# Taking the modulation products two pieces at a time, their matmuls in a fixed unbroken order

## The chip, the cores and the metric

The kernel runs on one core of one Trainium2 chip. The metric is the device time of one execution in microseconds. A core has engines that run side by side, each through its own queue in order: PE (TensorE, matrix products), PEld (PE's weight loads), DVE (VectorE), ACT (ScalarE), POOL (GpSimd) and SP (SyncE, which here issues nearly all DMA transfers).

## The reference

Two groups of tokens, 128 context tokens and 256 latent tokens, pass through two layers with the same code and weights of their own. Each layer is modulated by six vectors, made from a condition of each group:

```python
mod = (jax.nn.silu(cond) @ lp["w_mod"] + lp["b_mod"])[:, None, :]      # w_mod: (1024, 6 * 1024)
sh1, sc1, g1, sh2, sc2, g2 = jnp.split(mod, 6, axis=-1)
h = rms_norm(x, lp["norm1"]) * (1 + sc1) + sh1
o, new_ctx = token_mixers(h, lp, ctx_cache, rope_a, rope_b)
x = x + g1 * o
h = rms_norm(x, lp["norm2"]) * (1 + sc2) + sh2
x = x + g2 * conv_ffn(h, lp)
```

`token_mixers` projects h to the inputs of three mixers and their gates: A, grouped-query attention; B, multi-head latent attention; C, a Hyena long convolution. Their outputs are projected, gated, added and projected once more. `conv_ffn` is a projection up to 2 x 2816 columns, a convolution of width 3, a SiLU gate and a projection down. The change is in the first line alone, the products of `cond` with `w_mod`.

## The kernel before

All 384 tokens are kept as one batch in SBUF, turned so that channels lie on partitions. Each main product is exact to fp32 through a split: a weight is cut into a high and a low part (`hi_lo`: ACT copies the high part, DVE subtracts it), the tokens too, and `mm3` issues three matmuls (lines 269, 270, 271) for one product. An output of 128 columns of a projection from 1024 channels is 8 x 3 = 24 matmuls.

Weights come through two rings. `raw_ring` has 2 buffers of 1 MB, filled by SyncE's DMA (line 249 in `load_w`); from there a weight is split into `hi_ring` and `lo_ring`, which have 4 places each (a 1 MB load fills two). A load waits until the buffer that it takes, two loads back in the ring, has been read: by the split, when a main weight lies in it, and by its matmuls, when a piece of modulation weights lies in it.

The six vectors (v = 0 to 5) of a layer are made by `mod_vec`. A vector's 1024 x 1024 weights come in 4 pieces of 1 MB, of 256 rows (`mod_load`, line 329). For each piece PE runs 4 matmuls (line 338) of 32 columns each, side by side on the four column strips of its array (`tile_position`), in fp32, which the trace shows as two instructions each: x8 is a piece. They add into one PSUM bank; when all pieces are in, ACT copies the bank, PE transposes it (line 302), DVE adds the bias. `mod_vec` is a generator: it yields after each piece, after the copy, and at the end, so a vector is 4 + 2 steps. Some pieces are loaded ahead into other buffers (`ready`); the others go through `raw_ring`: 16 pieces of layer 0 (v = 2 to 5), and in layer 1 two of v = 0 and 1, four of v = 3 and four of v = 4.

`weave(main, (line, rate), ...)` takes a step of the main line and then, for each side line, adds the rate to a counter and takes a step when the counter reaches 1; the counters start at zero in each call. The modulation line `md` has rate R_MD. In each layer the main lines are, in order: the two halves of `hyena_in` (12 and 13 steps; three loads each), `attn_proj` (24 steps, nine matmuls to a step, six loads with the columns in widths of 512, 448 and 480), and then gates (16 steps, four loads) and branch (8 steps, four loads of 512 KB) for mixers 2, 0 and 1. Beside them run the Hyena chain `ch` up to the end of `attn_proj`, and the attention line `att` in gates and branches. `finish(md)` takes what is left before the output projection.

What the generators give is program order. Each engine's own order is fixed when the kernel is built: an instruction that is ready goes by priority, which is program order unless `tc.high_priority(offset=...)` raises it. `tc.issue_after(ins)` lets an instruction go to its engine only behind `ins`. The attention outputs (line 954) use both already:

```python
with ExitStack() as order:
    order.enter_context(tc.high_priority(offset=U_AV))
    if last is not None:
        order.enter_context(tc.issue_after(last))
    last = pe.matmul(p[b:b + 64, u], v, pT, start=start, stop=stop, tile_position=(0, b)).ins
```

Of the kernel before, what the change touches and what calls it, by code (L numbers as in the profile page):

```python
# [15 lines left out]
KD = 8  # L16
# [12 lines left out]
PI_C = TWO_PI - PI_A - PI_B  # L29
MAGIC = 12582912.0  # L30
ATT_LAG = 3
R_MD, R_FL, R_CH = 0.24, 2, 0.8
R_AT = 0.8, 0.9, 0.9, 1, 2
R_FL2, R_AH = 0.45, 0.5
PS_HY0 = {"mm": "123", "tr": "46", "fl": "05"}
# [11 lines left out]
U_AV = 2000  # L47
# [138 lines left out]
def kernel(  # L186
# [8 lines left out]
    act, dve, pool, pe, sp = nc.scalar, nc.vector, nc.gpsimd, nc.tensor, nc.sync  # L195
# [11 lines left out]
    def banks(**lines):  # L207

        for line, own in lines.items():
            turns[line] = [int(b) for b in own]  # L210

    def ps_of(line, *shape):
        own = turns[line]
        own.append(b := own.pop(0))
        n = 1
        for d in shape:
            n *= d
        v = all_banks[:, b, 0:n]
        if len(shape) == 1:
            return v  # L220
        return v.rearrange("p (a b) -> p a b", a=shape[0])
# [8 lines left out]
    def copy_a(out, in_, scale=1.0):  # L230
        act.activation(out=out, in_=in_, func=AF.Copy, scale=scale)  # L231
# [5 lines left out]
    def tt(out, a, b, op):  # L237
        dve.tensor_tensor(out=out, in0=a, in1=b, op=op)  # L238

    def stt(out, a, s, b, op0, op1):  # L240
        dve.scalar_tensor_tensor(out=out, in0=a, scalar=s, in1=b, op0=op0, op1=op1)  # L241

    raw_ring = Ring(base, 2, 2048)
# [41 lines left out]
    cT = base.alloc(KD, 32).ap()  # L285
# [14 lines left out]
    def transpose(out, in_):  # L300
        n = in_.shape[0]
        pe.transpose(out, in_, ident[:n, :n])  # L302
# [23 lines left out]
    def mod_load(l, v, k, buf):  # L326
        raw = buf.ap(2, 1024)
        src = w_mod[l, k * 256:(k + 1) * 256, v * 1024:(v + 1) * 1024]
        sp.dma_start(out=raw, in_=src.rearrange("(k p) n -> p k n", p=128))
        return raw  # L330

    def mod_vec(l, v, ready=(), bufs=()):

        gv = ps_of("md", 512)
        for k in range(KD // 2):
            raw = ready[k] if k < len(ready) else mod_load(l, v, k, raw_ring.get())
            for j in range(4):
                pe.matmul(  # L338
                    gv[32 * j:32 * j + 32], cT[:, 2 * k + j // 2], raw[:, j // 2, (j % 2) * 512:(j % 2) * 512 + 512],
                    start=k == 0, stop=k == KD // 2 - 1, tile_position=(0, 32 * j),  # L340
                )
            if bufs:
                bufs.pop(0).free()
            yield
        ms = mod_s
        copy_a(ms.ap(), gv)
        yield
        pm = ps_of("md", 4, 128)
        for q in range(4):
            transpose(pm[:, q], ms.ap()[:, q * 128:(q + 1) * 128])  # L350
        sums_of = pm.rearrange("p q (h j r) -> p h j q r", h=2, r=32)[:, :, :, :, 0:2]
        out = mods[l][:, v * 8:v * 8 + 8].rearrange("p (j q) s -> p j q s", q=4)
        bias = vecs[l][:, V_B + v * 8:V_B + v * 8 + 8].rearrange("p (j q) -> p j q", q=4)
        tt(out, sums_of[:, 0], bias.unsqueeze(3).to_broadcast([128, 2, 4, 2]), ALU.add)
        tt(out, out, sums_of[:, 1], ALU.add)
        if v in (1, 4):
            o = (V_N1, V_N2)[v // 4]
            g = vecs[l][:, o:o + 8].unsqueeze(2).to_broadcast([128, 8, 2])
            stt(avs[l][:, v // 4], mods[l][:, v * 8:v * 8 + 8], 1.0, g, ALU.add, ALU.mult)
        yield  # L360
# [895 lines left out]
    nxt = []  # L1256
# [36 lines left out]
    class Ahead:  # L1293


        def __init__(self, l, vs, n):
            ready = {v: [] for v in vs}
            bufs = {v: [] for v in vs}

            def loads():  # L1300
                for v, k in [(v, k) for v in vs for k in range(KD // 2)][:n]:
                    bufs[v].append(FA.alloc(2048, top=True))
                    ready[v].append(mod_load(l, v, k, bufs[v][-1]))
                    yield

            self.loads = loads()
            self.steps = chain(*[mod_vec(l, v, ready[v], bufs[v]) for v in vs])
# [36 lines left out]
    def chain(*lines):  # L1344
        for g in lines:
            yield from g
# [27 lines left out]
    ready = [mod_load(0, 0, k, early[k]) for k in range(2)]  # L1374
# [6 lines left out]
    for k in range(4):  # L1381
        ready.append(mod_load(0, 1, k, early[4 + k]))
    act.activation(out=cT[:, :, 0:2], in_=cT[:, :, 0:2], func=AF.Silu)
    weave(chain(mod_vec(0, 0, ready[:4]), mod_vec(0, 1, ready[4:])), (fl, R_F0), (squares(), 1.2))
    for b in early_parts:
        b.free()
    parts = split_slab.whole(F32R).cut(1024)
# [9 lines left out]
        sp.dma_start(out=rope_b[:, i], in_=rt[:, 128:192].rearrange("p (a b) -> p a b", a=2))  # L1397
    sp.dma_start(out=vecs[1], in_=p_vec[1])
    for l in range(NL):
        md = chain(*[mod_vec(l, v) for v in (2, 3, 4, 5)]) if l == 0 else chain(nxt.pop().steps, mod_vec(l, 4))  # L1400
        banks(**PS_HY0)
        weave(main, (md, R_MD), (fl, R_FL))
        finish(fl)
# [199 lines left out]
```

## Time and profile before

| | |
|---|---|
| time, median of 3 runs | 1503.31 us (1502.71 to 1505.6) |
| the profiled execution: time | 1507.35 us |
| its span, first to last instruction | 1505.2 us |
| its mean granted TensorE clock | 0.992 |
| PE busy | 1460.2 us, 97% of the span |
| DVE, ACT busy | 1005.3 us (67%), 750.7 us (50%) |
| HBM traffic over the span | 140 GB/s |

Busy time is time in which an instruction of the engine runs; matmuls overlap in the engine's pipeline, so a matmul's own duration is longer than its distance from the next. The granted clock is a share of TensorE's full speed, 2.4 GHz. In the lists, `banks` is PSUM, `base` the slab with the raw ring, `split` the slab with the split weights, `s` the slabs of temporary tiles; out<-in names what is written and read.

### The profile page before, as it was taken

Reading aid. Unit: us, or ns where it says so; the run is one execution under the profiler, and the core shown is the slowest. Engines: PE = TensorE matmul, PEld = TensorE weight load, DVE = VectorE, ACT = ScalarE, POOL = GpSimd, SP = SyncE. Lnnn points to the kernel's source line nnn. Section 1 sums busy time; section 2 is a strip of 40 time slices with the busy share of each in tenths; the row PEclk is TensorE's granted clock in tenths of the full one; section 3 lists DMA queues with packets and bytes.
Section 4 is the critical chain, followed back from the end, with each engine's and each line's share of the span. In section 5 each row is a group of like instructions: output and inputs, shape, how many; then the busy total and the mean of one; then the engine's idle time right before and its main releaser. Section 6 shows DMA issues by size and latency. Waiting matters only on the chain.

```text
span 1505.2 us, 22120 instructions
## 1 busy us (share of the span) xinstructions
PE 1460.2 (97%) x8574; PEld 1342.2 (89%) x8574; DVE 1005.3 (67%) x1920; ACT 750.7 (50%) x1376; POOL 97.1 (6%) x125
## 2 busy tenths in 40 slices
PE   5799999999999999999999999999999999999997
PEld 3589889989889899999997888999888989999997
DVE  5758569547447886686775766884655777567674
ACT  4644456455444663454545444855555464344343
POOL 0222210000000000000000212100000000000000
PEclk9899999999999999999999999999999999999999
DMA  9444354434466542343266345332333533433431
GB/s 366 146 134 157 135 164 140 114 105 126 140 211 233 191 134 95 125 126 128 85 226 220 124 142 180 103 102 88 90 122 114 184 110 113 139 102 122 156 116 52
DMA packets 177496, 212.84 MB, mean 141 GB/s; under 512 B 24176, under 2 KB 160112, under 8 KB 177392
## 3 DMA queue, kind: packets, MB, share of 16 engines
q1 hardware_dynamic: 176528, 206.99, 42.6%
q0 software_dynamic: 864, 4.46, 0.9%
q8 instruction: 67, 1.10, 0.3%
q14 instruction: 37, 0.30, 0.1%
HBM read 209.29 MB, written 2.13 MB: 140 GB/s over the span
## 4 chain that ended last, share of the span: by engine, by line
PE 92%; DVE 3%; ACT 2%; DMA 1%; issue 1%; SPq 0%; DVEq 0%; ACTq 0%
PE banks L269 27%; PE banks L270 26%; PE banks L271 26%; PE banks L302 3%; PE banks L338 3%; PE banks L922 3%; DVE s L238 2%; PE banks L954 2%; PE banks L558 1%; DMA base<-in_w_in_dram 1%; DVE split L235 1%; PE banks L503 1%; ACT s L231 1%; PE banks L538 0%; DMA s<-in_p_w_dram 0%
## 5 line engine op out<-in xcount | busy, mean ns | idle before, releaser
L231 ACT ACTIVATE split<-base 128x1024 fp32r<-128x1024 f32 (+2 forms) x272 | 280.8, 1040 | 374.1 <-PE banks L270 264.1
L235 DVE TENSOR_TENSOR split<-base,split 128x1024 fp32r<-128x1024 f32 (+2 forms) x272 | 332.0, 1225 | 181.4 <-ACT split L231 180.8
L269 PE MATMUL banks<-h,split 128*128 128x384 f32 x1280 | 432.9, 342 | 5.2 <-DVE h L403 3.6
L270 PE MATMUL banks<-h,split 128*128 128x384 f32 x1280 | 435.9, 341 | 0.3
L271 PE MATMUL banks<-h,split 128*128 128x384 f32 x1280 | 433.2, 339 | 0.0
L269 PEld LDWEIGHTS banks<-h,split 128*128 128x128 f32 x1280 | 241.4, 189 | 19.5 <-issue 8.4
L270 PEld LDWEIGHTS banks<-h,split 128*128 128x128 f32 x1280 | 242.1, 189 | 4.6 <-issue 1.6
L271 PEld LDWEIGHTS banks<-h,split 128*128 128x128 f32 x1280 | 241.6, 189 | 2.4 <-issue 0.7
L270 PE MATMUL banks<-s,split 128*128 128x384 f32 x672 | 225.8, 337 | 0.0
L271 PE MATMUL banks<-s,split 128*128 128x384 f32 x672 | 225.6, 338 | 0.0
L269 PE MATMUL banks<-s,split 128*128 128x384 f32 x672 | 223.2, 339 | 1.0 <-ACT s L231 0.8
L241 DVE SCALAR_TENSOR_TENSOR s<-banks,base,s 128x127 f32<-128x127 f32 (+1 forms) x448 | 172.6, 411 | 8.4 <-ACT s L417 4.3
L231 ACT ACTIVATE s<-banks 128x384 f32<-128x384 f32 (+11 forms) x212 | 94.4, 472 | 101.3 <-PE banks L271 38.7
L231 ACT ACTIVATE s<-s 128x384 fp32r<-128x384 f32 (+3 forms) x142 | 79.0, 562 | 103.9 <-DVE s L238 57.6
L269 PEld LDWEIGHTS banks<-s,split 128*128 128x128 f32 x672 | 125.6, 188 | 4.4 <-ACT s L231 1.4
L271 PEld LDWEIGHTS banks<-s,split 128*128 128x128 f32 x672 | 126.1, 188 | 2.0 <-DVE base L241 0.8
L270 PEld LDWEIGHTS banks<-s,split 128*128 128x128 f32 x672 | 126.2, 188 | 1.4 <-issue 0.2
L238 DVE TENSOR_TENSOR s<-banks,s 128x512 f32<-128x512 f32 (+3 forms) x132 | 81.6, 645 | 43.7 <-PE banks L271 18.8
L241 DVE SCALAR_TENSOR_TENSOR base<-banks,base 128x128 f32<-128x128 f32 (+1 forms) x128 | 46.9, 412 | 74.8 <-PE banks L271 74.8
L238 DVE TENSOR_TENSOR s<-s 128x256 f32<-128x256 f32 (+4 forms) x122 | 68.0, 568 | 23.6 <-ACT s L1225 8.3
L302 PE MATMUL banks<-base,s 128*128 128x128 f32 x442 | 75.3, 274 | 2.3 <-DVE s L241 1.3
L417 ACT ACTIVATE s<-banks,base 128x384 f32<-128x384 f32 x112 | 73.2, 655 | 7.1 <-PE banks L271 7.1
(145 smaller groups left out, 1729.7 us busy)
## 6 DMA issues: line engine op xcount, KB each, us to landing
base<-in_w_in_dram SPq DMA_DIRECT2D x40, 1024.0 KB, 5.4
base<-in_ffn_up_dram SPq DMA_DIRECT2D x40, 1024.0 KB, 5.2
base<-in_w_mod_dram SPq DMA_DIRECT2D x28, 1024.0 KB, 5.2
s<-in_w_mod_dram SPq DMA_DIRECT2D x14, 1024.0 KB, 7.5
base<-in_ffn_down_dram SPq DMA_DIRECT2D x16, 896.0 KB, 5.0
base<-in_w_branch_dram SPq DMA_DIRECT2D x24, 512.0 KB, 3.5
base<-in_w_out_dram SPq DMA_DIRECT2D x8, 1024.0 KB, 5.4
base<-in_ffn_down_dram SPq DMA_DIRECT2D x8, 1024.0 KB, 5.3
```

The costliest lines, as they stand in the source:

```text
L231: act.activation(out=out, in_=in_, func=AF.Copy, scale=scale)
L235: dve.tensor_tensor(out=lo, in0=src, in1=f(hi), op=ALU.subtract)
L238: dve.tensor_tensor(out=out, in0=a, in1=b, op=op)
L241: dve.scalar_tensor_tensor(out=out, in0=a, scalar=s, in1=b, op0=op0, op1=op1)
L269: pe.matmul(out, l[0], r[0], start=start, stop=False)
L270: pe.matmul(out, l[0], r[1], start=False, stop=False)
L271: pe.matmul(out, l[1], r[0], start=False, stop=stop)
L302: pe.transpose(out, in_, ident[:n, :n])
L338: pe.matmul(gv[32 * j:32 * j + 32], cT[:, 2 * k + j // 2], raw[:, j // 2, (j % 2) * 512:(j % 2) * 512 + 512], start=k == 0, stop=k == KD / ...
L417: act.activation(out=dst, in_=src, func=AF.Identity, scale=vec(l, w1), bias=vec(l, bias))
L922: pe.matmul(out, q_of(h)[:, i * 128:(i + 1) * 128], k, start=m == 0, stop=m == len(ks) - 1)
L954: last = pe.matmul(p[b:b + 64, u], v, pT, start=start, stop=stop, tile_position=(0, b)).ins
```

## The change

`mod_vec` gets a parameter `pieces`. With `pieces=2` it loads two pieces in one step and issues their 8 matmuls in one go, the piece that was loaded last first. In every call, also with one piece, the matmuls of a step go through `in_turn`: each but the first has its priority raised by U_AV = 2000 and is put behind the one before it. `pieces=2` is used for v = 2 to 5 of layer 0 and v = 4 of layer 1, where the line runs beside the main lines; R_MD goes from 0.24 to 0.16, as such a vector now takes 2 + 2 steps.

```diff
--- before.py
+++ after.py
@@ -29,7 +29,7 @@
 PI_C = TWO_PI - PI_A - PI_B
 MAGIC = 12582912.0
 ATT_LAG = 3
-R_MD, R_FL, R_CH = 0.24, 2, 0.8
+R_MD, R_FL, R_CH = 0.16, 2, 0.8
 R_AT = 0.8, 0.9, 0.9, 1, 2
 R_FL2, R_AH = 0.45, 0.5
 PS_HY0 = {"mm": "123", "tr": "46", "fl": "05"}
@@ -329,16 +329,34 @@
         sp.dma_start(out=raw, in_=src.rearrange("(k p) n -> p k n", p=128))
         return raw
 
-    def mod_vec(l, v, ready=(), bufs=()):
+    def in_turn(parts):
+
+        last = None
+        for part in parts:
+            with ExitStack() as order:
+                if last is not None:
+                    order.enter_context(tc.high_priority(offset=U_AV))
+                    order.enter_context(tc.issue_after(last))
+                last = part().ins
+
+    def mod_vec(l, v, ready=(), bufs=(), pieces=1):
 
         gv = ps_of("md", 512)
-        for k in range(KD // 2):
-            raw = ready[k] if k < len(ready) else mod_load(l, v, k, raw_ring.get())
-            for j in range(4):
-                pe.matmul(
-                    gv[32 * j:32 * j + 32], cT[:, 2 * k + j // 2], raw[:, j // 2, (j % 2) * 512:(j % 2) * 512 + 512],
-                    start=k == 0, stop=k == KD // 2 - 1, tile_position=(0, 32 * j),
-                )
+
+        def part(k, j, raw, first, last):
+            return pe.matmul(
+                gv[32 * j:32 * j + 32], cT[:, 2 * k + j // 2], raw[:, j // 2, (j % 2) * 512:(j % 2) * 512 + 512],
+                start=first, stop=last, tile_position=(0, 32 * j),
+            )
+
+        for k0 in range(0, KD // 2, pieces):
+            ks = range(k0, k0 + pieces)
+            raws = [ready[k] if k < len(ready) else mod_load(l, v, k, raw_ring.get()) for k in ks]
+            own = list(zip(ks, raws))[::-1]
+            in_turn([
+                lambda i=i, k=k, j=j, raw=raw: part(k, j, raw, k0 + i == 0, k0 + i == KD // 2 - 1)
+                for i, (k, raw) in enumerate(own) for j in range(4)
+            ])
             if bufs:
                 bufs.pop(0).free()
             yield
@@ -1397,7 +1415,10 @@
         sp.dma_start(out=rope_b[:, i], in_=rt[:, 128:192].rearrange("p (a b) -> p a b", a=2))
     sp.dma_start(out=vecs[1], in_=p_vec[1])
     for l in range(NL):
-        md = chain(*[mod_vec(l, v) for v in (2, 3, 4, 5)]) if l == 0 else chain(nxt.pop().steps, mod_vec(l, 4))
+        if l == 0:
+            md = chain(*[mod_vec(l, v, pieces=2) for v in (2, 3, 4, 5)])
+        else:
+            md = chain(nxt.pop().steps, mod_vec(l, 4, pieces=2))
         banks(**PS_HY0)
         weave(main, (md, R_MD), (fl, R_FL))
         finish(fl)
```

## Rows read from the trace of the kernel before

**Rows 1.** Part 1 of the page: busy time, share of the span, instructions of each engine.

```profile
PE 1460.2 (97%) x8574; PEld 1342.2 (89%) x8574; DVE 1005.3 (67%) x1920; ACT 750.7 (50%) x1376; POOL 97.1 (6%) x125
```

**Rows 2.** Part 4 of the page: the chain that ended last, shares by line.

```profile
PE banks L269 27%; PE banks L270 26%; PE banks L271 26%; PE banks L302 3%; PE banks L338 3%; PE banks L922 3%; DVE s L238 2%; PE banks L954 2%; PE banks L558 1%; DMA base<-in_w_in_dram 1%; DVE split L235 1%; PE banks L503 1%; ACT s L231 1%; PE banks L538 0%; DMA s<-in_p_w_dram 0%
```

**Rows 3.** Stages: window and length, busy us by engine (x instructions), granted clock, DMA share, GB/s.

```profile
142.00:207.00 65.00, 65.00 (x342) 51.31 (x341) 41.45 (x65) 24.25 (x45) 20.21 (x20) 1.00 0.48 156
...
367.00:430.00 63.00, 63.00 (x362) 51.33 (x361) 30.76 (x73) 30.98 (x72) 0.00 (x0) 1.00 0.41 125
```

**Rows 4.** The chain that ended last, in order of time: start us, us, what (x instructions).

```profile
95.70 0.98 PE banks L338 x4
...
388.76 3.18 PE banks L954 x32
...
836.82 0.97 PE banks L338 x2
840.25 0.99 PE banks L338 x6
...
1207.05 3.57 PE banks L338 x32
```

**Rows 5.** PE's timeline around a lone modulation piece: start us, us, engine line op.

```profile
117.49 0.33 PE L270 MATMUL banks<-h,split 128*128 128x384 f32 x1
117.67 0.34 PE L271 MATMUL banks<-h,split 128*128 128x384 f32 x1
117.94 1.06 PE L338 MATMUL banks<-base 128*32 128x512 f32 x8
118.93 0.45 PE L269 MATMUL banks<-h,split 128*128 128x384 f32 x1
119.21 0.34 PE L270 MATMUL banks<-h,split 128*128 128x384 f32 x1
```

**Rows 6.** Source line L338: what its engine sat idle for (us, times).

```profile
  DMA base<-in_w_mod_dram: 0.9, 2
```

**Rows 7.** Waits of SyncE's queue: who for whom, us in total, times, longest.

```profile
SPq L249 <- DVE split L235: 460.4, 74, 20.7
...
SPq L249 <- PE banks L338: 68.2, 15, 8.6
```

**Rows 8.** The chain in order of time again, behind the modulation run at 321.44.

```profile
322.49 5.56 DMA base<-in_w_in_dram
...
329.10 1.05 ACT split L231
```

**Rows 9.** DMA issues, 437.2 to 437.8: tile, queue, count, KB each, median us to landing.

```profile
base<-in_w_out_dram SPq DMA_DIRECT2D x2, 1024.0 KB, 6.6
```

**Rows 10.** Stages again: the projection's second width (layer 0), its third (layer 1).

```profile
163.11:182.79 19.68, 19.68 (x112) 16.30 (x111) 10.64 (x16) 7.06 (x15) 6.65 (x6) 1.00 0.55 193
...
923.56:943.72 20.16, 20.16 (x112) 17.95 (x110) 16.11 (x25) 9.60 (x21) 3.63 (x5) 1.00 0.51 147
```

**Rows 11.** Part 5 of the page, the weight split on DVE: busy, mean ns, idle before.

```profile
L235 DVE TENSOR_TENSOR split<-base,split 128x1024 fp32r<-128x1024 f32 (+2 forms) x272 | 332.0, 1225 | 181.4 <-ACT split L231 180.8
```

**Rows 12.** DMA issues of the attention projection, layer 0, 142 to 207.

```profile
base<-in_w_mod_dram SPq DMA_DIRECT2D x4, 1024.0 KB, 5.2
```

**Rows 13.** Groups of instructions in the projection's third width, layer 1: busy, mean ns, idle.

```profile
L269 PE MATMUL banks<-s,s 128*128 128x256 f32 x12 | 3.5, 288 | 0.0
```

**Rows 14.** Stages again: PE's busy time and clock around three waits.

```profile
810.00:814.00 4.00, 2.54 (x16) 1.36 (x9) 4.00 (x10) 3.50 (x8) 0.00 (x0) 1.00 1.03 397
814.00:818.00 4.00, 4.00 (x26) 2.91 (x25) 3.71 (x9) 4.00 (x11) 0.00 (x0) 1.00 0.95 270
826.00:830.00 4.00, 2.15 (x13) 1.67 (x11) 3.98 (x8) 3.64 (x5) 0.00 (x0) 1.00 0.63 204
830.00:834.00 4.00, 4.00 (x15) 3.91 (x15) 3.48 (x8) 0.00 (x0) 1.73 (x3) 0.57 0.70 250
328.00:332.00 4.00, 3.55 (x19) 2.89 (x18) 2.77 (x6) 3.87 (x6) 0.00 (x0) 1.00 0.44 75
```

## The prediction

> **What bounds the kernel now.** Begin with the busy times: TensorE (PE) works in 97% of the span [rows 1], and the chain that ended last lies on PE nearly throughout, 79% of it on the three products of the split matmul and 3% on the modulation matmuls, L338 [rows 2]. The table by stage says how tight that is: in the attention projection of layer 0 PE is busy for 65.00 us of 65.00, in the last gates and branch of that layer for 63.00 of 63.00 [rows 3]. In these stages one microsecond less of PE work is one microsecond less of time, and one microsecond in which PE waits for a weight is lost. Both happen here, so the question is what each weighs.
>
> A modulation piece is 4 matmuls, shown as 8 instructions. The chain in order of time has one row for each unbroken run of them [rows 4]. Look at how little the length depends on the count: a run of 2 takes 0.97 us, one of 4 0.98, one of 6 0.99, and a run of 32, four whole pieces, 3.57. So a piece that other matmuls break in two is paid twice. The row of a first half (x4 at 95.70) is the first of these, the piece at 836.82 and 840.25 the last; counted over the list, 16 rows hold no multiple of 8 (x2 to x6, and one x28), they stand for 7 broken pieces, and there are 9 runs more than there need be.
>
> The PE timeline around a lone piece (x8) gives the whole price of a run [rows 5]: matmuls follow each other every 0.18 us (117.49 to 117.67), the last one before the run is followed after 0.27, the run holds PE for 0.99 (117.94 to 118.93), the first matmul behind it for 0.28 (to 119.21). That is 0.09 + 0.99 + 0.10 = 1.18 us, and 1.17 for half a piece. A further piece inside a run costs (3.57 - 0.99) / 3 = 0.86 us.
>
> **The change part by part.**
>
> Chaining. Each piece's or pair's matmuls follow one another without a break; the same device already holds the 32 instructions of the attention outputs together (L954, one row, 3.18 us [rows 4]), so I take it that it works. 9 runs x 1.17 = 10.5 us less. It cannot gain more; it gains nothing if the breaks remain.
>
> Pairing. 16 pieces of layer 0 and 4 of layer 1 become 10 runs of two. Two lone runs cost 2.36, one run of two 1.18 + 0.86 = 2.04: 0.32 each, 3.2 us in all. With the chaining 13.7 us. That a run's first matmul must now wait for the piece loaded last I price at nothing: over all runs PE's weight loads waited 0.9 us for a modulation load [rows 6], and the weights already split cover the rest.
>
> R_MD. A vector took 4 + 2 steps and takes 2 + 2, and 0.24 x 4/6 = 0.16: 25 main steps for a vector as before. No instruction is added, no load grows; ACT's copy and DVE's adds are the same. I price this at nothing: finish(md) keeps one step instead of two in layer 0.
>
> The weight ring. This is what the change costs. The ring has two 1 MB buffers. SyncE's load of the next weight waits for the vector split of the last one (74 times) or for a modulation run (15 times) [rows 7]. A single piece holds one buffer and leaves the other to the main weights; a pair holds both until its matmuls have run, and no weight behind it can start before. Its matmuls stand where program order puts them, so the weights at hand are then those already split. What a late load costs is seen at 322.49, where w_in waited for L338: 5.56 us for the load, then ACT's split of 1.05 before the first matmul [rows 8]. With 0.1 between them I take 6.7 us from a run's end to the next weight. Two such loads issued together land after 6.6 us in the median of the two [rows 9]; if the first takes the 5.5 of a lone one, the second takes 7.7.
>
> Counting the steps of the weave (the counter starts at zero in each call, a step every 6.25), the pairs fall: v2 at step 7 of either half of hyena_in, v3 (layer 0) and v4 (layer 1) at steps 13 and 19 of the attention projection, v4 in layer 0 at step 7 of branch 2 and of gates 0, v5 at steps 7 and 13 of gates 1.
>
> hyena_in: behind the pair stand at least 2.5 outputs of 24 matmuls, whose weights are already loaded. At 0.18 us a matmul these are 10.8 us, more than 6.7. Nothing is lost.
>
> Attention projection, both layers. It has six loads a0 to a5 of four steps each. A step took (19.68 - 2 x 1.2) / 8 = 2.2 us in the second width and 20.16 / 8 = 2.5 in the third [rows 10]. Call the end of the pair at step 13 X. Three steps of a3 are left (6.5 us); a4 is usable at X + 6.7, or at X + 8.9 if the other freed buffer, the one that the reversed order frees first, is filled ahead of it: PE loses 0.2 to 2.4. The next pair's second piece needs a4's buffer, free after both halves are split (two splits of ACT and the last of DVE at 1.2 [rows 11]: X + 5.6 + 3.3 = 8.9). It lands 5.2 us later [rows 12], at X + 14.1; PE ends step 19 at 6.7 + 3 x 2.5 = X + 14.2. The run of 2.0 ends at X + 16.2, and only then a5 may be loaded: usable at X + 22.9. PE has one step left, to X + 18.7, so it lacks 4.2 us; if the run comes one step later, 6.7. Behind this wait are a5's four steps, the copies of the projection, and all of the attention that reads them. What can fill it is the Hyena chain: 12 groups of three matmuls in the 20 us of this stage, 3.5 us for the first of each three [rows 13], tied to VectorE step by step. I let it fill 0.7 of the lesser wait, and take 3.5 us at a5 and 0.3 at a4 for each layer.
>
> Branch 2, gates 0, gates 1 at step 7. One output, or half of one, is left (2 us and the attention beside it), so 6.7 us leave 2 to 4 open. But at 322.49 the same wait cost PE 0.45 us (3.55 busy in the four from 328 [rows 14]), as the attention line filled the rest. I take 0.3 each, 0.8 together; the far end is 3 x 3 = 9 with no cover. Gates 1 at step 13 has 1.5 outputs left and a load of half the size: nothing.
>
> The clock. A wait has an afterpay. PE was idle for 1.46 us in 810 to 814 and its granted clock stayed at 1.00 (2.4 GHz) in the next 4; it was idle for 1.85 in 826 to 830 and got 0.57 in the next 4 us, most of them at the lower level of 1.2 GHz, which is 1.7 us of work lost [rows 14]. Whether a gap that the Hyena chain breaks up does the same these rows don't tell; between 0 and 1.7 I take half, 0.8 a layer. The Trainium skill (TensorE: Matmul & The Clock Gate, "HAM oscillation — how this bites in real kernels") says that a PE that waits for a DMA between bursts drops to the half clock and begins each burst cold. By that rule both waits would pay in full, and the sum below would be -1.9 us instead of -3.7; the row at 826 agrees with it, the one at 810 doesn't.
>
> Sum: -10.5 - 3.2 + 2 x (3.5 + 0.3 + 0.8) + 0.8 = -3.7 us. The profiled execution took 1507.35 us for a span of 1505.2; it becomes 1503.65. The median of the runs is 1503.31, 4.04 below that execution, and becomes 1499.6.
>
> **The rivals.**
>
> The waits are covered. If the Hyena chain and the next stage's ready work fill the attention projection's gaps too, what is left of the losses is 0 to 7 us and the time 1489.6 to 1496.6. For it: PE found work through nearly all of the wait at 322.49. Against: that was among attention heads; in the projection all later work needs a5.
>
> Gain and loss cancel: losses of 10.7 to 16.7 us, 1500.3 to 1506.3. The clock's full price (+1.8) alone leads here, 1501.4; it is what the Trainium skill's rule above gives. With it 2 us more at a4 in each layer make it no change at all.
>
> Slower: the wait for a5 and its like. With 6.7 unfilled at a5, 2.4 at a4 and 1.7 for the clock a layer pays 10.8, both 21.6, and with the 0.8 the whole is +8.7: 1512. It decides from 8 us a layer on, where the losses pass 16.7. The place is width three of the projection, in both layers.
>
> The change does not do what it says: matmuls of others still break the runs. Then the pairing's 3.2 stand against waits of 10: +6.8, 1510. L954's unbroken runs speak against it.
>
> **How the numbers follow.** About 0.2%, 3 us, is what a measurement of this kernel tells from no change. Forecast (losses of 7 to 10.7, 1496.6 to 1500.3): 0.28. Covered: 0.22. Cancelled: 0.26. Slower by waits: 0.21. Runs still broken: 0.03. So faster 0.50, same 0.26, slower 0.24. Cases of both signs hold much, so the range goes far to either side, 1490 to 1509: it leaves out the upper half of the slower cases, some 0.13, and little of the covered one, some 0.05. The forecast's own is 1496.6 to 1500.3.
>
> **What would show it.** Right: in the chain 10 rows of x16 near 1.9 us and no L338 row under x8 in the weaves; PE idle for 3 to 4 us before L269 late in the projection of each layer, ended by an ACT split behind a w_in load that waited for L338; a granted clock below 1.00 there. Wrong: runs still broken (the 10.5 gone); no idle time in the projection (then nearer 1490); idle time of over 8 us a layer, or new gaps in gates 0 and 1 (then slower); a modulation run that itself waits for its second piece.

## The result and the profile after

The changed kernel takes 1525.19 us (median of 4 runs, 1523.86 to 1529.78); beside it the kernel before took 1504.05 (4 runs, 1502.71 to 1505.6). The ratio is 1.0140 with a 95% interval of 1.0128 to 1.0153, so the change makes the kernel 21 us slower. The forecast was 1499.6 in a range of 1490 to 1509: the direction was wrong, and the time lies 16 us beyond the far end. The profiled execution of the changed kernel has a span of 1523.4 us against 1505.2, 18.2 more. Line numbers move: the modulation matmuls of L338 are now L347, the attention outputs of L954 are L972.

Start where the prediction started, with the busy times and the chain (part 1 of the page, the chain's lines of part 4, and of the groups by line the four of the modulation matmuls: busy us, mean ns, idle before):

```profile
PE 1458.2 (96%) x8574; PEld 1348.4 (89%) x8574; DVE 1000.6 (66%) x1920; ACT 744.2 (49%) x1372; POOL 98.7 (6%) x125
...
PE banks L269 26%; PE banks L270 25%; PE banks L271 25%; PE banks L302 3%; DMA base<-in_w_in_dram 2%; PE banks L940 2%; PE banks L347 2%; DVE s L238 2%; PE banks L972 2%; DVE split L235 1%; ACT split L231 1%; ACT s L231 1%; PE banks L576 1%; PE banks L521 1%; DVE s L241 1%
```

```profile
L347 PE MATMUL banks<-base 128*32 128x512 f32 x224 | 30.1, 632 | 0.0
L347 PE MATMUL banks<-s,base 128*32 128x512 f32 x112 | 13.1, 596 | 0.0
L347 PE MATMUL banks<-split,base 128*32 128x512 f32 x32 | 4.3, 604 | 0.0
L347 PE MATMUL banks<-h,base 128*32 128x512 f32 x16 | 2.1, 605 | 0.0
```

The gain is there. The same four groups of L338 had 39.4, 13.9, 4.3 and 2.1 us before, together 59.7; now they have 49.6. That is 10.1 less, and the 44 runs on PE have become 27: at the 0.19 us around a run that the forecast read from [rows 5], 17 x 0.19 = 3.2 more. So 13.3 us of PE work went, where 13.7 were forecast. But against [rows 1] PE's busy time fell by 2.0 alone, and span less busy time, PE's idle time, rose from 45.0 to 65.2. In the chain against [rows 2], transfers of w_in have gone from 1% to 2% and stand ahead of the attention outputs. Two things ate the gain: waits for weights, and matmuls that run at a lower clock behind them.

The stages say where (columns as in [rows 3]; boundaries are the first projection matmul of each stage). First the kernel before: the projection of layer 0, gates 0 with its branch in layer 0, the projection of layer 1.

```profile
141.84:210.10 68.26, 68.26 (x362) 54.31 (x362) 42.84 (x70) 26.93 (x51) 20.37 (x20) 1.00 0.50 162
...
272.30:343.62 71.32, 69.54 (x450) 62.05 (x450) 33.37 (x69) 37.33 (x76) 0.45 (x3) 1.00 0.41 114
...
882.42:943.72 61.30, 61.30 (x336) 51.46 (x334) 38.35 (x58) 25.08 (x47) 12.35 (x16) 1.00 0.55 178
```

Then the changed kernel: in layer 0 hyena_in, the projection, gates 0 with its branch, and all gates and branches together; in layer 1 hyena_in, the projection, gates and branches.

```profile
65.01:140.41 75.40, 75.34 (x450) 69.06 (x449) 50.64 (x99) 39.47 (x72) 17.62 (x22) 0.98 0.41 133
140.41:214.94 74.53, 68.90 (x371) 57.18 (x369) 43.59 (x73) 26.21 (x50) 14.38 (x19) 0.95 0.50 160
...
277.55:358.67 81.12, 71.69 (x440) 64.20 (x440) 36.12 (x70) 39.26 (x76) 0.45 (x3) 0.94 0.37 103
...
214.94:509.89 294.95, 282.93 (x1730) 253.38 (x1728) 177.35 (x351) 151.17 (x312) 5.06 (x9) 0.98 0.47 148
...
825.64:891.74 66.10, 63.87 (x392) 59.34 (x393) 48.73 (x96) 34.56 (x61) 12.97 (x18) 1.00 0.44 142
891.74:965.75 74.01, 68.32 (x371) 56.27 (x369) 42.00 (x69) 26.10 (x50) 16.18 (x18) 0.95 0.47 149
965.75:1233.13 267.38, 263.01 (x1623) 246.35 (x1623) 172.72 (x341) 148.25 (x306) 3.84 (x7) 1.00 0.39 118
```

| stage (PE idle in brackets), us | before | after |
|---|---|---|
| hyena_in, layer 0 | 75.99 (0) | 75.40 (0.1) |
| attention projection, layer 0 | 68.26 (0) | 74.53 (5.6) |
| gates and branches with the output projection, layer 0 | 285.55 (1.8) | 294.95 (12.0) |
| of these gates 0 and its branch | 71.32 (1.8) | 81.12 (9.4) |
| hyena_in, layer 1 | 70.24 (2.0) | 66.10 (2.2) |
| attention projection, layer 1 | 61.30 (0) | 74.01 (5.7) |
| gates and branches with the output projection, layer 1 | 272.16 (5.4) | 267.38 (4.4) |

PE did not wait at all in either projection before. Now it waits 5.6 us in each, and its granted clock there has fallen from 1.00 to 0.95. In layer 0 the rest of the loss lies in gates 0 and its branch, which take 9.8 us more; the other gates and branches of that layer give 0.4 us back.

**Layer 1's projection, one wait.** The chain in order of time, with three modulation runs ahead of it (start us, us, what; compare [rows 4]):

```profile
126.29 1.85 PE banks L347 x16
...
402.96 0.98 PE banks L347 x2
...
407.12 1.88 PE banks L347 x14
...
944.67 1.04 PE banks L347 x8
945.73 5.49 DMA base<-in_w_in_dram
951.24 1.06 ACT split L231
952.33 1.30 DVE split L235 x2
```

A pair is one run of 16 instructions in 1.85 us. Only one of the ten is broken, at 402.96, where the attention outputs came in behind its first matmul, which is not raised in priority. Now look at the run at 944.67: the transfer at 945.73 is released by its first half, eight instructions. The half that runs first reads the piece loaded last, so the buffer taken last comes free first. The two loads issued behind this run (issues from 945.6 to 946.2 and from 946.4 to 947; KB, us to landing):

```profile
base<-in_w_in_dram SPq DMA_DIRECT2D x1, 1024.0 KB, 5.5
...
base<-in_w_in_dram SPq DMA_DIRECT2D x1, 960.0 KB, 7.0
```

The 960 KB are a5, the last weights of this projection, and needed first. The 1024 KB are the first weights of the gates, needed later. They go first and land in 5.5 us; a5 is issued at 946.59, shares the transfer engines with them, and takes 7.0. PE and ACT show the end of it (start us, us, engine line op, in brackets the idle time before):

```profile
944.60 1.92 PE L347 MATMUL banks<-base 128*32 128x512 f32 x16
...
950.50 0.28 PE L271 MATMUL banks<-s,s 128*128 128x256 f32 x1
954.67 1.57 PE L269 MATMUL banks<-split,h 128*128 128x480 f32 x3 [3.89 <-ACT split L231]
```

```profile
951.24 2.00 ACT L231 ACTIVATE split<-base 128x1024 fp32r<-128x1024 f32 x2 [2.50 <-DMA base<-in_w_in_dram]
...
953.62 1.90 ACT L231 ACTIVATE split<-base 128x960 fp32r<-128x960 f32 x2
```

ACT splits the weights that nobody waits for (128x1024) and then a5's (128x960). The run ends at 944.60 + 1.85 = 946.45; PE's first matmul with a5 is at 954.67, 8.2 us later. In layer 0 the same pair of loads goes out at 193.63 (1024 KB) and 194.49 (960 KB, again 7.0 us), and there ACT's split of the gates' weights ran from 199.11 on, two copies followed, and a5's split came at 202.06.

**Gates 0 of layer 0** show another form of the same hold. SyncE's queue (start us, us, line, x transfers):

```profile
279.92 0.37 SPq L329 DMA_DIRECT2D base<-in_w_mod_dram  x1
282.78 3.03 SPq L1081 DMA_DIRECT2D base<-in_mla_w_uq_dram  x6
...
314.37 0.37 SPq L329 DMA_DIRECT2D base<-in_w_mod_dram  x1
321.28 1.43 SPq L1081 DMA_DIRECT2D base<-in_mla_w_uq_dram  x3
322.76 0.49 SPq L249 DMA_DIRECT2D base<-in_w_in_dram  x1
```

The pair's first piece takes one ring buffer at 279.92 and holds it until the run at 320.19, for 40 us. The other goes to weights of the attention line (line 1081), which are split only just before 314.37; then the second piece is loaded. Behind it in the queue stand the attention line's next weights and w_in, which go out at 321.28 and 322.76. Before, w_in had gone out at 287.42 and the second part of w_uq at 298.07. Over the whole run loads of line 249 wait for a modulation run 19 times, 22.8 us at the longest; in [rows 7] it was 15 times and 8.6 us. The total is 67.6 against 68.2 us, so what tells is where the waits fall. The wait is in PE's timeline (the row at 322.98 is the last work before it):

```profile
322.98 0.60 PE L302 MATMUL banks<-base 128*128 128x128 f32 x4
329.82 0.69 PE L269 MATMUL banks<-h,split 128*128 128x384 f32 x1 [6.24 <-ACT split L231]
```

In the kernel before, PE spent the same wait for w_in (from 322.49 on, [rows 8]) on the matmuls of this second part of w_uq, 27 of the following kind, and its weights had come through the ring at 298.07:

```profile
323.43 0.34 PE L269 MATMUL banks<-s,s 128*128 128x384 f32 x1
```

Here too the clock falls with the wait. Windows of 4 us behind the waits of layer 0's projection, of gates 0 and of layer 1's projection, columns as before; the first number behind the length is PE's busy time, the third from the end its clock (compare [rows 14]):

```profile
200.00:204.00 4.00, 1.82 (x5) 1.30 (x5) 3.80 (x5) 3.94 (x6) 0.65 (x1) 0.60 0.35 106
204.00:208.00 4.00, 4.00 (x17) 3.69 (x16) 3.07 (x5) 0.38 (x1) 0.00 (x0) 0.55 0.98 272
...
324.00:328.00 4.00, 0.00 (x0) 0.00 (x0) 0.24 (x2) 0.00 (x0) 0.00 (x0) 0.88 0.98 286
328.00:332.00 4.00, 2.18 (x6) 1.74 (x7) 2.20 (x2) 3.06 (x3) 0.00 (x0) 0.50 0.21 44
332.00:336.00 4.00, 4.00 (x20) 4.00 (x19) 1.43 (x2) 0.00 (x0) 0.00 (x0) 0.76 0.67 183
...
948.00:952.00 4.00, 2.16 (x13) 1.55 (x12) 1.56 (x5) 1.39 (x2) 0.07 (x1) 0.96 1.06 384
952.00:956.00 4.00, 1.33 (x3) 1.05 (x4) 3.67 (x5) 3.41 (x5) 0.00 (x0) 0.50 0.27 86
956.00:960.00 4.00, 3.98 (x14) 3.03 (x13) 2.09 (x3) 0.00 (x0) 0.00 (x0) 0.68 0.98 277
```

0.50 is the lower level, 1.2 GHz. An estimate of what it costs is the busy time of a window times the missing share of its clock: 0.73 + 1.80 = 2.5 us behind the wait in layer 0's projection, 1.09 + 0.96 = 2.1 in gates 0, and 0.09 + 0.67 + 1.27 = 2.0 in layer 1's projection.

### The profile page after: what moved, and what is told of

Read it like the earlier page. It is cut to its first block, busy times and chain, and to the rows that moved or that the text cites. A ratio compares the mean times of both kernels' runs of the same rounds, so it can differ in the third digit from the quotient of the medians.

```text
span 1523.4 us, 22120 instructions
## 1 busy us (share of the span) xinstructions
PE 1458.2 (96%) x8574; PEld 1348.4 (89%) x8574; DVE 1000.6 (66%) x1920; ACT 744.2 (49%) x1372; POOL 98.7 (6%) x125
## 4 chain that ended last, share of the span: by engine, by line
PE 88%; DVE 4%; DMA 3%; ACT 3%; issue 1%; POOL 0%; SPq 0%; DVEq 0%; ACTq 0%; POOLq 0%
PE banks L269 26%; PE banks L270 25%; PE banks L271 25%; PE banks L302 3%; DMA base<-in_w_in_dram 2%; PE banks L940 2%; PE banks L347 2%; DVE s L238 2%; PE banks L972 2%; DVE split L235 1%; ACT split L231 1%; ACT s L231 1%; PE banks L576 1%; PE banks L521 1%; DVE s L241 1%
## 5 line engine op out<-in xcount | busy, mean ns | idle before, releaser
L235 DVE TENSOR_TENSOR split<-base,split 128x1024 fp32r<-128x1024 f32 (+2 forms) x272 | 328.1, 1211 | 173.0 <-ACT split L231 172.3
L238 DVE TENSOR_TENSOR s<-banks,s 128x512 f32<-128x512 f32 (+3 forms) x132 | 81.5, 646 | 44.7 <-PE banks L271 21.7
L235 DVE TENSOR_TENSOR s<-s,s 128x384 fp32r<-128x384 f32 (+2 forms) x102 | 62.8, 619 | 28.3 <-ACT s L231 20.7
```

What stands on the lines that cost most here:

```text
L235: dve.tensor_tensor(out=lo, in0=src, in1=f(hi), op=ALU.subtract)
```

## The experiments

The main theory: a pair holds both ring buffers until its run, and the reversed order then gives the buffer of the less urgent load back first. Rivals: the chaining itself costs (raised priority, matmuls put behind one another); the slower pace or the two steps in one do; or one stage alone pays. Each ratio is to the kernel before, timed on the same chip, whose median was 1504.87 for the first four runs, 1504.22 for the next four and 1505.74 for the last two.

**Chaining alone.** All pieces single, in their runs unbroken.

```diff
-R_MD, R_FL, R_CH = 0.16, 2, 0.8
+R_MD, R_FL, R_CH = 0.24, 2, 0.8
...
-            md = chain(*[mod_vec(l, v, pieces=2) for v in (2, 3, 4, 5)])
+            md = chain(*[mod_vec(l, v) for v in (2, 3, 4, 5)])
...
-            md = chain(nxt.pop().steps, mod_vec(l, 4, pieces=2))
+            md = chain(nxt.pop().steps, mod_vec(l, 4))
```

> Each piece alone as before (one piece to a step, R_MD 0.24), but its matmuls chained. Theory (the loss is the ring held by pairs): PE's time in modulation runs falls by some 9 of the 69.6 us of the kernel before, PE's idle time stays near 32 us, and the time is 1504 - 10 = 1494 us (1490 to 1497). Rival (the chaining itself does the harm, by pulling modulation matmuls ahead of work that the chain of the end needs): 1510 to 1525. Second rival (the new order of the schedule alone moves the time by up to 1%): anywhere from 1494 to 1515, with idle time in other places than after.

Measured: 0.9979 (0.9969 to 0.9988), 1501.87 us. The modulation matmuls take 50.8 us in 36 runs, 8.9 less, and with 8 x 0.19 around the runs 10.4 less: the forecast's term for the chaining, 10.5, is right as PE work. (The 69.6 and 32 us that the expectation gives for the kernel before are 59.7, or 68.1 with the 0.19 around each run, and 45.0 in its trace.) As time it is not: the expected 1490 to 1497 was missed. PE's idle time rose from 45.0 to 47.6 and the span fell by 6.0 (to 1499.2); the median fell by 3.0 alone (1.8 to 4.7 by the interval), as the traced execution of the kernel before lies 2.5 us above its median (1507.35 against 1504.87). So the chaining by itself doesn't cost, but of 10.4 us of PE work it gives some 3 us of time.

**Pairs in loading order.** The reversal is taken out.

```diff
-            own = list(zip(ks, raws))[::-1]
+            own = list(zip(ks, raws))
```

> The changed kernel, but a pair's matmuls go in the order of loading, so that the buffer of the piece loaded first comes free first, and with it the load that PE needs first. Theory (part of the loss is that the weight needed second is loaded and split ahead of the one needed first): in the projection of each layer a5 is loaded first, PE resumes 1.5 to 3 us earlier, in both layers together with the clock 4 to 8 us less, 1517 to 1521 us. Rival (the order of loading makes no difference, both loads go together): 1524 to 1526. If the run now breaks after the first piece, because the second has not landed, the gain is smaller and single runs show.

Measured: 0.9996 (0.9987 to 1.0006), 1504.07 us. One slice costs 21.7 us (1.0140 against 0.9996). The time is far below the 1517 to 1521 expected. Layer 0's projection takes 64.09 us with no idle time. Layer 1's is still long, with 2.95 us of idle time; there the pair at 923.23 came as one run of 16.

```profile
874.29:942.39 68.10, 65.15 (x366) 54.51 (x364) 40.31 (x66) 26.45 (x50) 17.26 (x19) 1.00 0.50 162
```

Two things change at once, though: in loading order the first piece's matmuls can run as soon as it has landed, so its buffer comes back before the second piece is even in, and the order of the freed buffers is mended. The hold-forward run below parts them.

**Pairs in loading order, not chained.**

```diff
-                if last is not None:
-                    order.enter_context(tc.high_priority(offset=U_AV))
-                    order.enter_context(tc.issue_after(last))
...
-            own = list(zip(ks, raws))[::-1]
+            own = list(zip(ks, raws))
```

> Pairs as in the changed kernel, in the order of loading, without the chain (no raised priority, no issue order). Theory (the ring alone makes the loss): the idle time of the changed kernel in the projections and gates 0 stays (some 15 to 20 us over before), the modulation runs break again and cost 6 to 12 us more than in the changed kernel: 1527 to 1535 us. Rival (the chain makes the loss): 1500 to 1510.

Measured: 1.0048 (1.0031 to 1.0065), 1511.27 us; the modulation matmuls are back at 59.1 us. Against the run before, the chaining is worth 7.8 us among pairs. Pairing without it is a loss, but a smaller one than the expected 1527 to 1535: the expectation had counted on the changed kernel's idle time, most of which is not there in loading order (50.2 us in all, against 65.2).

**Pairs as changed, the second piece in a buffer of its own.** The order within the run and its wait for both pieces stay; in nine of ten pairs the second piece goes into a free place of the activations' memory instead of the ring.

```diff
+OWN_FROM = 1
...
-            raws = [ready[k] if k < len(ready) else mod_load(l, v, k, raw_ring.get()) for k in ks]
...
+                    if pieces == 2 and k > k0 - 1 + OWN_FROM:
+                        try:
+                            b = FA.alloc(2048, top=True)
...
+                    if b is None:
+                        b = raw_ring.get()
+                    else:
+                        held.append(b)
+                    raws.append(mod_load(l, v, k, b))
```

> The changed kernel, but the second piece of each pair lies in a buffer of its own from the arena, wherever there is room for 1 MB (9 of the 10 pairs; not the first of v = 4 in layer 0), so that a pair holds one buffer of the weight ring, as a single piece does. Theory (the ring): the idle time of the two projections and of gates 0 goes (14 of the 20 us that the change added), the clock stays at 1.00 there, and the time is 1490 to 1500 us. Rival (long runs or the new order of the schedule make the loss): 1515 to 1526.

Measured: 0.9944 (0.9929 to 0.9959), 1495.88 us. This is the clearest run, as expected: the changed kernel, with its order and its unbroken runs, becomes 29 us faster and beats the kernel before once the pair holds one ring buffer instead of two. With one buffer in the ring there is also no wrong order of release left, so this run does not part the hold from the order. Its page and its windows (both projections, and gates and branches of layer 0 between them):

```profile
PE 1446.9 (97%) x8574; PEld 1342.0 (90%) x8574; DVE 1001.9 (67%) x1920; ACT 748.8 (50%) x1376; POOL 100.8 (7%) x125
```

```profile
139.11:203.43 64.32, 64.32 (x364) 54.25 (x363) 42.87 (x65) 26.46 (x50) 18.18 (x20) 1.00 0.52 171
203.43:489.08 285.65, 281.23 (x1745) 253.09 (x1743) 179.25 (x357) 154.69 (x317) 4.75 (x9) 0.99 0.48 153
...
871.07:934.44 63.37, 63.37 (x356) 53.57 (x355) 40.09 (x62) 26.36 (x51) 18.29 (x19) 1.00 0.49 158
```

The projections take 64.32 and 63.37 instead of 74.53 and 74.01, with PE busy throughout and the clock at 1.00. Span for span, the changed kernel's 30.4 us more (1523.4 against 1493.0) are 10.2 in layer 0's projection, 9.3 in its gates and branches, 10.6 in layer 1's projection, and 0.3 in all the rest.

**Hold kept, order mended.** The run begins with one matmul (column strip 0) of the last piece, so it still waits for both pieces; then comes the whole first piece, then the rest of the last.

```diff
-            own = list(zip(ks, raws))[::-1]
+            own = list(zip(ks, raws))
+            turns = [(k, j, raw) for k, raw in own for j in range(4)]
+            if pieces > 1:
+                turns.insert(0, turns.pop(4))
...
```

> The changed kernel, but of a pair's unbroken run the last piece's first strip goes first, then the whole first piece, then the rest of the last. So the run waits for both pieces as in the changed kernel and stays in one, but the buffer of the first piece comes free first, which the next weight needs. Theory A (what costs is that both buffers are held until the second piece has landed): the time stays within 4 us of the changed kernel's 1525, 1521 to 1526. Theory B (what costs is that the weight needed second is loaded and split first): most of the 21 us that the order of loading gave back come back here too, 1504 to 1512. Between them both have a part.

Measured: 1.0077 (1.0056 to 1.0099), 1515.79 us, between the two theories: both have a part. In layer 1's projection a5 now goes first: the loads issued from 941 to 943 (each with the us to its landing), and PE from the run on.

```profile
base<-in_w_in_dram SPq DMA_DIRECT2D x1, 1024.0 KB, 8.2
base<-in_w_in_dram SPq DMA_DIRECT2D x1, 960.0 KB, 5.4
```

```profile
939.54 1.93 PE L347 MATMUL banks<-base 128*32 128x512 f32 x16
...
948.02 0.92 PE L269 MATMUL banks<-split,h 128*128 128x480 f32 x3 [1.78 <-ACT split L231]
```

a5 lands in 5.4 us, the gates' weights in 8.2. From the run's end at 941.4 to a5's first matmul are 6.6 us, the forecast's 6.7; PE's idle time is 3.1 us in this stage and 3.5 in layer 0's. So the order is worth 9.4 us of the 21 (median 1525.19 to 1515.79; 9.5 by the ratios, give or take 4 by their intervals), and the rest, some 12 us (1.0077 against 0.9996), is the hold. In gates 0 it is the hold above all: there PE is still idle for 5.12 us in one wait, where it was 6.24.

**Pairs apart.** Two pieces are loaded in one step, at the changed pace, but each is a run of its own, in loading order (`joint` is false in every call).

```diff
-            own = list(zip(ks, raws))[::-1]
-            in_turn([
+            own = list(zip(ks, raws))
+            if joint:
+                own = own[::-1]
+            turns = [
...
+            for some in (turns,) if joint else (turns[:4], turns[4:]):
+                in_turn(some)
```

> Two pieces to a step and R_MD 0.16 as in the changed kernel, but each piece's matmuls are a chain of their own, in the order of loading, so the first piece's buffer is given back as soon as its own matmuls are done. Theory A (held buffers): no waits of the changed kernel, runs of single pieces: 1500 to 1506 us, near the chain alone. Rival (the pace, two pieces at one step of the weave, makes the loss): 1515 to 1526.

Measured: 0.9982 (0.9971 to 0.9993), 1501.25 us. The pace of 0.16 and the loads of two pieces in one step cost nothing: as expected, the time equals that of chaining alone (0.9979) within the intervals. This kernel is the base of the next two.

**Joint pairs in the projections only** (v = 3 of layer 0, v = 4 of layer 1; the other pairs apart), and **joint pairs in the gates only** (v = 4 and 5 of layer 0). The edits are shown against the kernel with all pairs apart.

```diff
-            md = chain(*[mod_vec(l, v, pieces=2, joint=v in ()) for v in (2, 3, 4, 5)])
+            md = chain(*[mod_vec(l, v, pieces=2, joint=v in (3,)) for v in (2, 3, 4, 5)])
...
-            md = chain(nxt.pop().steps, mod_vec(l, 4, pieces=2, joint=False))
+            md = chain(nxt.pop().steps, mod_vec(l, 4, pieces=2, joint=True))
```

> As the last one, but the pairs that fall into the attention projections (v = 3 of layer 0, v = 4 of layer 1) are the changed kernel's unbroken reversed pairs. Theory: the loss of the two projections comes back alone, PE idle some 5 us in each and the clock low behind it: 9 to 13 us a layer over the kernel with all pairs apart, 1518 to 1530 us if that is at 1502; at least + 12. Rival (the losses of the changed kernel hang together, a shifted schedule rather than single places): no such sum.

```diff
-            md = chain(*[mod_vec(l, v, pieces=2, joint=v in ()) for v in (2, 3, 4, 5)])
+            md = chain(*[mod_vec(l, v, pieces=2, joint=v in (4, 5)) for v in (2, 3, 4, 5)])
```

> The same with the unbroken reversed pairs for v = 4 and 5 of layer 0 alone, which fall beside branch 2, gates 0 and gates 1. Theory: the one loss of gates 0 comes back, some 6 us of idle PE and 3 to 5 of clock, + 8 to 12 us over the kernel with all pairs apart. Rival (in the attention stages the attention line covers the wait, as I predicted, and gates 0 lost its time through the earlier shift): + 0 to 2.

Measured: 1.0047 (1.0032 to 1.0062), 1511.37 us, and 1.0041 (1.0026 to 1.0056), 1510.72 us. On the same chip the pairs apart took 1501.25, so the projections' pairs cost 10.1 us and the gates' 9.5. The gates' loss came as expected; the projections' did not: 10.1 for both layers, where the theory asked for 9 to 13 in each. The windows of the kernel with pairs in the projections (layer 0's, its gates and branches, layer 1's), then those of the one with pairs in the gates (layer 0's gates and branches):

```profile
139.42:214.28 74.86, 69.44 (x377) 57.49 (x377) 45.19 (x73) 27.65 (x52) 15.94 (x20) 0.95 0.46 147
...
214.28:495.22 280.94, 278.04 (x1731) 249.64 (x1730) 176.03 (x351) 150.50 (x312) 5.10 (x9) 1.00 0.49 156
...
877.06:950.92 73.86, 68.35 (x370) 56.23 (x368) 42.55 (x71) 26.59 (x53) 16.18 (x18) 0.95 0.46 149
```

```profile
202.32:500.68 298.36, 285.11 (x1756) 254.85 (x1754) 181.89 (x359) 156.10 (x319) 7.88 (x11) 0.99 0.46 149
```

With pairs apart these stages took 63.32, 288.30 and 66.38 us. The first kernel reproduces both long projections, but its gates and branches of layer 0 are 7.4 us shorter: part of a projection's loss is given back in the next stage, probably as it finds its weights loaded. The second reproduces the long gates, 10.1 us more, and leaves layer 0's projection at 63.32. Together they make 19.6 of the 23.9 us between pairs apart and the changed kernel.

**Both kinds of run with buffers of their own.** First, chaining alone with 23 of 24 ring pieces moved out of the ring; then the changed kernel with both pieces of a pair moved out where there was room (14 of 20 pieces).

```diff
+                    if pieces == 1 and not ready:
+                        try:
+                            b = FA.alloc(2048, top=True)
...
```

> Single chained pieces, R_MD 0.24, but each piece that went through the weight ring gets a buffer of its own from the arena (23 of the 24 that go beside the main lines have room), so modulation pieces hold no ring buffer at all. Theory: runs cost 10 us less than before, as with the chain alone, and the main weights' lookahead is never cut: 1490 to 1498 us, below the chain alone at 1502. Rival (what the chain alone did not give, it lost to the new order and not to the ring): 1500 to 1504.

```diff
-OWN_FROM = 1
+OWN_FROM = 0
```

> The changed kernel with both pieces of a pair in arena buffers where there is room (14 of 20 pieces; in most of the other pairs one piece is still in the ring). Theory: as with the second piece alone in its own buffer, 1492 to 1497 us, the runs at some 56 us of PE. Rival (arena buffers come free late, so that the pieces are loaded late and the run holds up what follows): 1500 to 1510.

Measured: 0.9933 (0.9916 to 0.9949), 1494.77 us, and 0.9926 (0.9912 to 0.9941), 1494.88 us. Both came as expected and beat the kernel before by 10 to 11 us, and the intervals overlap: once the modulation pieces are out of the ring, pairing adds nothing that these runs can tell. The first of them is 6.9 us below chaining alone on the ring (0.9933 against 0.9979), and 5.3 of that is idle time: span less busy time is 1492.4 - 1450.1 = 42.3 us, against 47.6. So single pieces in the ring cost time too; that the kernel before loses by them as well is likely, but no run takes them out of its ring without the chaining.

## Why the prediction was wrong

**The gain was right as PE work, not as time.** "9 runs x 1.17 = 10.5 us" measured 10.4 in the run with chaining alone; chaining and pairing together, forecast at 13.7, measured 13.3. A little of that is luck: 8 runs went, from 44 to 36, not 9, as the x4 at 788.21 and the x28 behind it make two runs in either kernel. But the forecast took each us of PE work for a us of time ("one microsecond less of PE work is one microsecond less of time"), and there this step failed: chaining alone shortened the kernel by 3.0 us, and by 10 only when the pieces left the ring (0.9933). The step that took L954's device to hold was right but for one pair, whose first matmul is not raised. Pace and steps, priced at nothing, cost nothing (pairs apart). hyena_in, whose pairs (v = 2, layer 0) were priced at nothing, shows next to no loss: 75.40 us with 0.1 of it idle, 75.99 before and 74.40 with the second piece in its own buffer.

**The attention projection: a step that failed.** The forecast took "6.7 us from a run's end to the next weight" at a5, and from it 3.5 + 0.3 us of waiting a layer. The text had seen that the reversed order frees the wrong buffer first and used it at a4, where it set 0.2 to 2.4; at a5, where PE has no step left to hide it, it kept 6.7. The traces show 8.2 there, with a5 at 7.0 us behind the gates' weights at 5.5. With the order mended the same interval is 6.6 and PE's idle time 3.1 and 3.5 us a layer: the forecast of 3.8 comes near a kernel whose freed buffers come in the order in which the weights are needed. With the reversal it is 5.6. PE also had no step of a4 left when the run came; the text gave that as a bound ("if the run comes one step later, 6.7") and did not take it. Against that the cover was put too low: of layer 1's 8.2 us PE was idle for 4.5, so the Hyena chain and transposes filled 3.7, not 0.7. That the idle time is not further off is luck, two errors against each other.

**The clock, taken at half.** 0.8 us a layer were forecast, between 0 and 1.7. The windows give 2.0 us behind layer 1's wait and 2.5 in layer 0, both above that far end. That the Hyena chain breaks up the gap did not protect the clock: in layer 0 the longest single gap is 1.98 us, and the clock fell to 0.60 and 0.55 behind it. The rule of the Trainium skill (TensorE: Matmul & The Clock Gate, "HAM oscillation — how this bites in real kernels"), which the forecast quoted and followed only in a rival, is that a PE waiting for a DMA between bursts falls to the half clock and begins each burst cold. All three waits shown here agree with it; the shorter one at 810 in [rows 14], which left the clock at 1.00, does not.

**Gates and branches: "0.3 each", "as the attention line filled the rest".** This failed worst, and in one place, gates 0; branch 2 and gates 1 lost next to nothing, as forecast. The forecast listed who waits for a pair's buffers, but counted main weights only. The attention line's own weights pass the same two buffers and the same queue; at 314 to 322 they stood behind the pair as well, so the cover starved with what it should cover, and PE did nothing for 6.24 us. The row that the forecast read the cover from, 322.49, was filled by just these weights' matmuls. Forecast 0.8, bound 9; measured 9.3 against the kernel with the second piece apart, 9.5 by the run with pairs in the gates only.

**The sum.** By the spans, and with the kernel that keeps the second piece out of the ring as the dividing line: a gain of 12.2 us (1505.2 to 1493.0; forecast 13.7) and a loss of 30.4 (forecast 10.0). By the medians they are 9.0 and 29.3, and that the gain comes out near the forecast is luck in part, as this kernel also frees ring buffers. A projection costs 10.4 us more by its stage, close to the 10.8 of the rival that ends slower; that rival kept the gates at 0.8, for 8.7 us in all. Put the gates at 9.3 and it gives 8.7 + 8.5 = 17.2 us; the span grew by 18.2 and the median by 21. From the other side, pairs apart, the terms weigh differently: 7.5 us of the chaining's gain missing, the two projections' pairs 10.1 together, net of what later stages give back, the gates' 9.5. In both accounts the gates are off by 9 us, and the losses came together. The range treated them as separate mishaps, while both follow from the one cause, two buffers held at once; so the range was too short.

**What stays open.** The two partial runs leave 4.3 of 23.9 us unexplained, little more than their intervals allow (some 4 us). The pairs of v = 2 in hyena_in, which neither contained, make at most 0.9 of it (75.40 us against 74.49 with pairs apart). More lies in the gates and branches of layer 0, where the two parts act on each other: 7.4 us less with the one, 10.1 more with the other, but 6.7 more with both. A ring of three buffers, the plainest test of the hold, wasn't tried; a single buffer beside the ring already found no room at one pair of ten. Where the rest of the chaining's 10.4 us went is not shown in full. And the windows don't tell how much of a projection's 10.4 us beyond 5.6 of idle time and 2.0 to 2.5 of clock is work moved from the stage behind; the 7.4 us given back in the projections-only run say that some of it is.

## What to carry to other kernels

Before several loads are made to wait for one consumer, count the buffers of the ring that they pass, who else loads through it, and how long each is held: here pairing saved some 3 us of PE work over chaining alone and made the kernel 23 us slower than that, as a pair is the whole ring. In such a ring the order in which a consumer releases its buffers is the order in which the next loads are issued; release first what the urgent load will take. When a stall is priced as covered by another line of work, check that this line's own inputs don't stand behind the same wait.

## What the runs showed of the hardware

Of two loads of about 1 MB issued 0.5 to 0.9 us apart on one queue, in the three cases read here (5.4 and 7.0 in layer 0) the first took about as long as the load in [rows 8] (5.4 to 5.5 us against 5.56), and the second took 7.0 to 8.2: the later one paid for the sharing. A pair that was broken behind 2 of its 16 instructions took 0.98 + 1.88 us instead of 1.85, so even two instructions paid the whole price of a run. Behind waits of 3.9 and 6.2 us PE ran at a granted clock of 0.50, and was back at 1.00 in the window from 960 and from 336 on: about 2 us lost for each wait, besides the wait. A gap that short matmuls broke into pieces of under 2 us did the same in layer 0's projection.
